# Dilated attention: masked keys give their place to the neighbouring block's keys, two row tiles per turn, the farthest keys merged in the last pass

## The chip, the cores and the metric

The kernel runs on one core of a Trainium2 chip. The metric is the time of one execution on the device in microseconds (us), the median of several runs. "Granted clock" is the share of TensorE's full speed that the chip granted in a stretch.

## The reference

One layer of a decoder with two parallel branches on 2048 tokens of width 1024. Cut to what matters here:

```python
z = rmsnorm(h) @ w_in                  # q | k | v | gate_b | u | v_a | gate_a
q, k = rope(rmsnorm(q)), rope(rmsnorm(k))          # 8 heads of 64
for window, r in ((128, 1), (512, 4), (2048, 16)):  # dilation r
    # query t sees keys t - r*j for j = 0 .. window/r = 128, where they exist
    scores = where(band, q @ [k_prev | k_own].T / 8, -1e30)
    out, lse = softmax(scores) @ [v_prev | v_own], logsumexp(scores)
o = sum over the three of softmax(lse) * out
mixed = concat(o * silu(gate_b), gmlp(u, v_a) * silu(gate_a))
h = h + mixed @ w_out
h = h + sigmoid(rmsnorm(h) @ w_ple_gate + b) * (p @ w_ple_proj)
```

Within a residue class of the dilation the tokens lie in blocks of 128. Query i of a block sees keys 0 to i of its own block and keys i to 127 of the block before. So there are 129 keys, and the one at position i of the block before is the farthest. With dilation 16 there is one block per class and no block before.

## The kernel before

Everything is float32 in accuracy: each operand of a product is split into a high and a low part, and three products are summed. The work is cut into 16 row tiles of 128 tokens and goes in three passes; the results between the passes go through DRAM.

**Pass 1** (`prep`, `step`, `post_qk`, `post_v`, `post_gb`) normalises each row tile, turns it and projects it to q, k, v and gate_b: 24 matmuls of 512 columns each per group. q and k are scaled and rotated (buffers `m1`, `m2`, two of each; `sq`, one), split to fp16 and stored; v is stored as fp16 parts.

**Pass 2** is the attention, with PE's order written by hand. For each pair of heads (`hp`, four of them) and each dilation (`br`, in the order 0, 2, 1), a `Step` does `scores` (TensorE, then the mask, the negated maximum and exp), `turn` (split of the weights to fp16 high and low, one DMA transpose to `pt`) and, `LAG_C` steps later, `values`. A step whose query tile has a block before it has 256 columns of scores per head, two heads, so 512 columns; where there is none, two query tiles share a step. That is 152 steps. Between the steps `fill` places the gMLP branch's products, 1.3 us of them per step. All attention outputs with their denominators and maxima go to `d_o` (`ob` reads them back).

**Pass 3** runs per row tile n: `mixed(n)` (L572) loads the three branches' results (`ob`), the gate product and the gMLP result (`ma`, `mg`) and calls `merge` (L545): DVE works out the weights `w` and scales `ob`, POOL adds the three branches and multiplies by the gate into `ma`. `turn_mixed` (L587) turns `mg` and then `ma` by DMA through the buffer `tm` and splits the result to `aT`. `out_proj(n)` (L596) does 48 matmuls and adds to `xt`. `norm3(n)` (L904) normalises `xt` into `xn`, turns it through `turned` in place (`norm_T` L206, `turn_rows` L197, `turn_words` L172: ACT copies out of `xn`, the DMA transposes back into `xn`, DVE copies out of `xn`) and splits the result. `gate(n)` (L909) does the last 60 matmuls and stores. Tiles 0 and 1 are turned by TensorE and not by DMA.

The order of instructions on each engine and queue in passes 1 and 3 is set by a planner that may issue what is ready ahead of what stands before it in the program. Tiles of one name in one pool share that name's buffers: a new one takes a buffer over from an older one when all that touches the older one is done. `xn`, `ob`, `ma`, `mg`, `tm` and `turned` have one buffer each. The loop of pass 3, in the order of the program:

```python
        for n in range(NT):
            if n + 1 < NT:
                out_proj(n + 1)
            if n + 1 < NT:
                norm3(n + 1)
                load_p(n + 1)
            if n + 2 < NT:
                prep3(n + 2)      # mixed(n + 2), turn_mixed(n + 2)
            gate(n)
```

Of the kernel before, what the change touches and what calls it, by code (L numbers as in the profile page):

```python
# [13 lines left out]
I32 = mybir.dt.int32  # L14
U16 = mybir.dt.uint16
# [4 lines left out]
S = 2048  # L20
# [16 lines left out]
def _shape_constants():  # L37

    p = np.arange(128)

    def mask(keys, back=False):
        keep = keys[None, :] >= p[:, None] if back else keys[None, :] <= p[:, None]
        return np.where(keep, 0, NEG).astype(np.float32)
    k0 = p.reshape(32, 4).T.reshape(128)
    return {"c_ident": np.eye(128, dtype=np.float32),
            "c_mask": np.concatenate([mask(k0, True), mask(k0), mask(p, True), mask(p)], 1),
            "c_freq": INV_FREQ.reshape(1, 32)}
# [3 lines left out]
PR, PH, OB, SV = 3, 6, 5, 5  # L51

LAG_B, LAG_C = 1, 6

BLOCK0, FILL = 18, 1.3
# [26 lines left out]
def hybrid_layer(ctx: ExitStack, tc: tile.TileContext, io, out):  # L82
# [11 lines left out]
    d_qk = [dram.tile([128, HEADS, S], F16, name=f"d_{n}") for n in "qk"]  # L94
# [3 lines left out]
    d_gb = dram.tile([S, 512], F32, name="d_gb")  # L98
    d_at = dram.tile([NT, 128, D], F32, name="d_at")
# [5 lines left out]
    cst.tile([128, 16], F32, name="pad")  # L105
# [163 lines left out]
    with ExitStack() as s1, ExitStack() as s1q:
# [90 lines left out]
        def v_scale():  # L360
# [3 lines left out]
            ones = p1.tile([128, 128], F32, name="ones")  # L364
# [37 lines left out]
        def post_qk(n, which, ps):  # L402
# [17 lines left out]
            nc.vector.tensor_tensor(r, r, rs[:, :, None].to_broadcast([128, HEADS, 64]), op=OP.mult)  # L420
            hl = p1.tile([128, HEADS, 2, 64], F16, name="hl", bufs=2)
# [4 lines left out]
        def turn_qk(n, which, hl):  # L426
# [8 lines left out]
            nc.sync.dma_start(d_qk[which][:, :, n * 128:(n + 1) * 128], st)  # L435

        def post_v(n, ps):
# [4 lines left out]
            nc.scalar.activation(vt[:, :, 0, 0:64], z, AF.Copy, scale=sv)  # L442
            nc.vector.scalar_tensor_tensor(vt[:, :, 1, 0:64], z, sv, vt[:, :, 0, 0:64],
# [513 lines left out]
```

## Time and profile before

| | us |
|---|---|
| three runs | 1290.10, 1296.17, 1296.32 |
| median | 1296.17 |
| the profiled execution | 1295.01 |
| its span, first to last instruction | 1293.2 |
| TensorE's granted clock over the span | 0.976 |
| busy over the span: PE / DVE / ACT / POOL | 1201.3 / 888.2 / 648.9 / 512.1 |

The profile's page gives busy times, a map of 40 slices and the chain that ended last. Times in the rows are microseconds from the start of the span. A row of the timeline is one instruction or a run of equal ones: start, length, engine, line, operation, what it writes and reads. "Idle before" in square brackets is how long the engine had waited and for whom.

### The profile page before, as it was taken

Reading aid. Unit: us, or ns where it says so; the run is one execution under the profiler, and the core shown is the slowest. Engines: PE = TensorE matmul, PEld = TensorE weight load, DVE = VectorE, ACT = ScalarE, POOL = GpSimd, SP = SyncE. Lnnn points to the kernel's source line nnn. Section 1 sums busy time; section 2 is a strip of 40 time slices with the busy share of each in tenths; the row PEclk is TensorE's granted clock in tenths of the full one; section 3 lists DMA queues with packets and bytes.
Section 4 is the critical chain, followed back from the end, with each engine's and each line's share of the span. In section 5 each row is a group of like instructions: output and inputs, shape, how many; then the busy total and the mean of one; then the engine's idle time right before and its main releaser. Section 6 shows DMA issues by size and latency. Waiting matters only on the chain.

```text
span 1293.2 us, 21329 instructions
## 1 busy us (share of the span) xinstructions
PE 1201.3 (93%) x7166; PEld 976.0 (75%) x7166; DVE 888.2 (69%) x2253; ACT 648.9 (50%) x1273; POOL 512.1 (40%) x454
## 2 busy tenths in 40 slices
PE   5999999989995799899799799879999999999998
PEld 4778877767884687687687688768778888888887
DVE  5885565655575678778778678598766766666733
ACT  5754334334344577677677677444334434434422
POOL 4852343433453456555555565342212121221100
PEclk9999999999997899899999999989999999999999
DMA  7598777776769899999999999955555655654531
GB/s 263 160 229 197 168 183 166 165 180 157 175 171 239 202 202 220 219 216 236 218 217 223 219 229 215 207 176 174 141 147 123 165 156 128 153 162 127 143 90 49
DMA packets 442254, 233.21 MB, mean 180 GB/s; under 512 B 337440, under 2 KB 392864, under 8 KB 442144
## 3 DMA queue, kind: packets, MB, share of 16 engines
q1 hardware_dynamic: 442144, 231.85, 75.4%
q8 instruction: 56, 0.92, 0.3%
q14 instruction: 54, 0.44, 0.1%
HBM read 102.66 MB, written 57.28 MB: 124 GB/s over the span
## 4 chain that ended last, share of the span: by engine, by line
PE 41%; DMA 19%; DVE 16%; ACT 7%; issue 7%; POOL 6%; SPq 4%; DVEq 0%; ACTq 0%; POOLq 0%
PE mm L227 17%; PE mm L627 8%; PE gt L227 5%; DMA pt<-raw 4%; DMA xt<-raw 3%; PE s L227 3%; DMA st<-hl 3%; PE s L755 3%; PE pt L791 2%; DVE aT L194 2%; DMA ob<-d_o 2%; ACT raw L179 2%; POOL rsh L148 2%; DVE m L420 1%; DVE pr L758 1%
## 5 line engine op out<-in xcount | busy, mean ns | idle before, releaser
L227 PE MATMUL mm<-wslot,aT 128*128 128x512 f32 x1536 | 362.8, 392 | 7.8 <-ACT aT L193 3.3
L227 PEld LDWEIGHTS mm<-wslot,aT 128*128 128x128 f32 x1536 | 289.4, 189 | 70.4 <-ACT aT L193 4.6
L627 PE MATMUL mm<-wslot,aT 128*128 128x512 f32 x1152 | 317.9, 418 | 23.2 <-DVE raw L618 14.2
L627 PEld LDWEIGHTS mm<-wslot,aT 128*128 128x128 f32 x1152 | 214.1, 197 | 63.5 <-DVE raw L618 14.6
L114 POOL TENSOR_TENSOR raw<-pr,raw 128x512 f16<-128x512 f32 (+1 forms) x152 | 178.0, 1177 | 151.6 <-ACT raw L773 137.9
L766 ACT ACTIVATE pr<-pr,ost 128x256 f32<-128x256 f32 (+1 forms) x384 | 150.5, 451 | 78.8 <-DVE ost L764 70.9
L227 PE MATMUL gt<-wslot,aT 128*128 128x512 f32 x744 | 177.8, 393 | 6.1 <-DVE gb L452 5.3
L227 PEld LDWEIGHTS gt<-wslot,aT 128*128 128x128 f32 x744 | 139.8, 189 | 38.0 <-DVE gb L452 7.0
L791 PEld LDWEIGHTS <-pt 128*128 128x128 f16 x1800 | 66.3, 99 | 62.1 <-issue 33.7
L773 ACT ACTIVATE raw<-pr 128x512 f16<-128x512 f32 (+1 forms) x152 | 93.2, 620 | 39.6 <-DMA pt<-raw 37.4
L791 PE MATMUL pt<-sv,pt 128*128 128x65 f16 x1800 | 83.6, 196 | 21.8 <-DMA pt<-raw 21.8
L758 DVE CUSTOM_DVE_ANT_0 pr<-s,mask 128x256 f32<-128x256 f32 (+1 forms) x256 | 81.3, 359 | 29.7 <-POOL raw L114 16.0
L227 PE MATMUL av<-wslot,aT 128*128 128x512 f32 x360 | 86.0, 392 | 7.3 <-DVE gb L452 6.3
L227 PE MATMUL s<-wslot,aT 128*128 128x512 f32 x384 | 90.0, 390 | 1.6 <-POOL wslot L135 1.6
L114 POOL TENSOR_TENSOR m<-m,m 128x512 f32<-128x512 f32 x32 | 47.9, 1498 | 94.8 <-DVE rsh L147 88.8
L227 PEld LDWEIGHTS av<-wslot,aT 128*128 128x128 f32 x360 | 67.2, 188 | 23.6 <-DVE gb L452 7.9
L227 PEld LDWEIGHTS s<-wslot,aT 128*128 128x128 f32 x384 | 72.0, 188 | 17.0 <-POOL wslot L135 2.0
L755 PEld LDWEIGHTS <-sq 128*128 128x128 f16 x768 | 70.4, 121 | 13.7 <-issue 7.4
L755 PE MATMUL s<-sk,sq 128*128 128x256 f16 (+1 forms) x512 | 73.7, 279 | 7.0 <-DMA sk<-d_k 6.1
L566 POOL TENSOR_TENSOR ma<-ob,ma 128x512 f32<-128x512 f32 x16 | 24.5, 1533 | 122.1 <-DMA ma<-d_gb 58.0
L563 POOL TENSOR_TENSOR ob<-ob 128x512 f32<-128x512 f32 x16 | 21.0, 1314 | 126.5 <-DVE ob L561 126.5
L764 DVE TENSOR_SCALAR ost<-ost 128x2 f32<-128x2 f32 (+1 forms) x152 | 66.9, 442 | 2.6
(209 smaller groups left out, 1723.4 us busy)
## 6 DMA issues: line engine op xcount, KB each, us to landing
xt<-x SPq DMA_DIRECT2D x32, 512.0 KB, 4.6
d_o<-ost SPq DMA_DIRECT2D x48, 264.0 KB, 3.2
raw<-w_in SPq DMA_DIRECT2D x38, 256.0 KB, 3.7
sv<-d_vt SPq DMA_DIRECT2D x32, 264.0 KB, 3.5
ob<-d_o SPq DMA_DIRECT2D x16, 528.0 KB, 4.6
xt<-d_at SPq DMA_DIRECT2D x16, 512.0 KB, 5.0
out<-th SPq DMA_DIRECT2D x32, 256.0 KB, 2.8
d_at<-raw SPq DMA_DIRECT2D x28, 256.0 KB, 2.5
```

Source lines behind the costliest of these rows:

```text
L114: nc.gpsimd.tensor_tensor(dst, a, b, op=op)
L148: nc.gpsimd.tensor_tensor(dst, dst, mhalf[:, :width], op=OP.pow)
L179: nc.scalar.activation(turned[t].bitcast(U16), words[:, t], AF.Copy)
L194: nc.vector.tensor_tensor(lo, f, hi.bitcast(F32), op=OP.subtract)
L227: nc.tensor.matmul(ps, aT[:, ha, k, :], w(slot, hw, k), start=(n == 0), stop=(n == 3 * nk - 1))
L627: nc.tensor.matmul(ps, GT[c][:, ha, k, :], slots[g][:, hw, k, :], start=(n == 0), stop=(n == 23))
L755: nc.tensor.matmul(ps[:, c:c + nk], cols(br, j, Q[h]), cols(br, j, K, n, h, self.nb), start=(n == 0), stop=(n == 1))
L758: nc.vector.tensor_tensor_reduce(pr[:, c:c + nk], ps[:, c:c + nk], mask[:, m - nk:m], -1.0, 3e38, op0=OP.add, op1=OP.min, accum_out=o[:, j ...
L764: nc.vector.tensor_scalar(nm, nm, math.log(PSCALE), None, op0=OP.add)
L766: nc.scalar.activation(pr[:, c:c + nk], pr[:, c:c + nk], AF.Exp, bias=o[:, j - j0, 130 + h:131 + h], scale=-1.0)
L773: nc.scalar.activation(ph, pr[:, :width], AF.Copy)
L791: nc.tensor.matmul(PO[0][:, j % 2, h], self.pt[:, t, c // 128], vt[:, h, vv, 0:65], start=(n == 0), stop=(n == 3 * self.nb - 1))
```

## The change

The scores of a query tile with a block before it are still computed for 256 keys per head, but the keys of its own block that the mask excludes are overwritten in PSUM with the scores of the same positions in the block before (`copy_predicated`). So one tile of 128 keys per head holds all keys but the farthest. Two query tiles now make one `Pair`, with one split and one DMA transpose of 512 weights. For the values the turned weights must be parted again: an AND on DVE with a table of bits gives the own block's share (`pc`), a subtraction on POOL leaves the neighbour's share in `pt`; this comes `LAG_P` = 6 steps behind, five tiles behind the pair, and the values come 9 steps behind. All scores steps have one query tile: 192 of them, 96 pairs, of which 56 are parted. The gMLP filling per step is 0.9 us (no block before) or 1.13 us.

The farthest key's score is a plain dot product: `far_scores` in pass 1 multiplies q with the k of 1 and of 4 row tiles before on POOL and sums on DVE. For this k and v are also stored in float32 (`d_kr`, `d_vr`). `merge` in pass 3 takes these two as two more branches: `mixed` loads the two v tiles into `vr`, POOL multiplies each by its weight and adds it. `vr` takes the buffer of `xn`.

`spatial_weights` of the gMLP moves from the start of pass 2 to row tile 3 of pass 1 and goes through DRAM (`d_ws`). q and k lie in DRAM and in `sk` in blocks of 512 tokens, loaded with 4 transfers each instead of 6.

```diff
-PR, PH, OB, SV = 3, 6, 5, 5
-LAG_B, LAG_C = 1, 6
-BLOCK0, FILL = 18, 1.3
+PR, PH, PC, OB, SV = 3, 4, 2, 5, 5
+LAG_B, LAG_P, LAG_C = 1, 6, 9
+BLOCK0, FILL = 18, (0.9, 1.13)
...
+    FAR = 1, 4
...
             nc.vector.tensor_tensor(r, r, rs[:, :, None].to_broadcast([128, HEADS, 64]), op=OP.mult)
+            if which:
+                nc.sync.dma_start(d_kr[n * 128:(n + 1) * 128], f1)
+            RT["qk"[which]] = n, f1
...
+        def far_scores(n):
+            far = small.tile([128, 2, HEADS], F32, name="far", bufs=1)
+            if n < FAR[1]:
+                nc.vector.memset(far, -NEG)
+            for x, back in enumerate(FAR):
+                if n >= back:
+                    t = p1.tile([128, HEADS, 64], F32, name="m2", bufs=2)
+                    f = t.rearrange("p h d -> p (h d)")
+                    k = RT["k"]
+                    if n - back == k[0]:
+                        k = k[1]
+                    else:
+                        k = f
+                        nc.sync.dma_start(f, d_kr[(n - back) * 128:(n - back + 1) * 128])
+                    pool_tt(f, k, RT["q"][1], OP.mult)
+                    nc.vector.tensor_reduce(far[:, x], t, axis=AX.X, op=OP.add, negate=True)
+            nc.sync.dma_start(d_far[n], far)
...
             nc.scalar.activation(vt[:, :, 0, 0:64], z, AF.Copy, scale=sv)
+            vr = p1.tile([128, 512], F32, name="sq")
+            nc.scalar.activation(vr, ps, AF.Copy, scale=sv)
+            nc.sync.dma_start(d_vr[n * 128:(n + 1) * 128], vr)
...
         nc.gpsimd.tensor_tensor(o, o, nums[:, 4:8], op=OP.add)
         nc.gpsimd.tensor_tensor(o, o, nums[:, 8:12], op=OP.add)
+        for x, back in enumerate(FAR):
+            if n < back:
+                continue
+            t = vr[:, 512 * x:512 * x + 512].rearrange("p (q h d) -> p q h d", q=4, h=2)
+            nc.gpsimd.tensor_tensor(t, t, w[:, 3 + x][:, :, :, None].to_broadcast([128, 4, 2, 64]), op=OP.mult)
+            nc.gpsimd.tensor_tensor(o, o, t, op=OP.add)
         m = mx.rearrange("p (q h d) -> p q h d", q=4, h=2)
         nc.gpsimd.tensor_tensor(m, o, m, op=OP.mult)
...
         nc.sync.dma_start(mx[0], d_gb[rows])
-        merge(ob, mx[0])
+        vr = pm.tile([128, D], F32, name="xn")
+        for x, back in enumerate(FAR):
+            if n >= back:
+                nc.sync.dma_start(vr[:, 512 * x:512 * x + 512], d_vr[(n - back) * 128:(n - back + 1) * 128])
+        merge(ob, mx[0], n, vr)
...
+        class Pair:
+            def turn(self):
+                pr = self.pr.rearrange("p i h k -> p (i h k)")
+                hl = stage().bitcast(F16).rearrange("p (t c) -> p t c", t=2)
+                nc.scalar.activation(hl[:, 0], pr, AF.Copy)
+                pool_tt(hl[:, 1], pr, hl[:, 0], OP.subtract)
+                pt = p2.tile([128, 8, 128], F16, name="pt", bufs=PH)
+                nc.sync.dma_start_transpose(pt, hl.rearrange("p t c -> p (t c)"))
...
+            def part(self, br, after):
...
+                with tc.issue_after(after.ins):
+                    nc.vector.tensor_tensor(d, a, bits[:, None, None, m:m + 64].to_broadcast([128, 2, 2 * n, 64]),
+                                            op=OP.bitwise_and)
+                pool_tt(a, a, d, OP.subtract)
...
+                top = o[:, j - j0, 130:132]
+                if nb == 2:
+                    own = ps[:, :, 128:256]
+                    nc.vector.copy_predicated(own, m.bitcast(U32)[:, None].to_broadcast([128, 2, 128]),
+                                              ps[:, :, 0:128])
+                    nc.vector.tensor_reduce(top, own, axis=AX.X, op=OP.max, negate=True)
...
+                self.last = nc.vector.tensor_scalar(top, top, math.log(PSCALE), None, op0=OP.add)
+                for h in range(2):
+                    nc.scalar.activation(pr[:, h], own[:, h], AF.Exp, bias=top[:, h:h + 1],
+                                         scale=1.0 if nb == 2 else -1.0)
...
+                    for w, v in zip((self.pair.pc, self.pair.pt) if self.nb == 2 else (self.pair.pt,), self.v):
```

## Rows read from the trace of the kernel before

**Rows 1.** The page's map of 40 slices, TensorE's line (tenths busy).

```profile
PE   5999999989995799899799799879999999999998
```

**Rows 2.** Table by stretch: length, busy time and count per engine, clock, DMA share, GB/s.

```profile
0.00:400.00 400.00, 370.32 (x1602) 300.69 (x1602) 253.05 (x454) 183.78 (x312) 183.18 (x173) 1.00 0.75 187
400.00:424.40 24.40, 10.43 (x44) 8.30 (x44) 15.45 (x26) 9.96 (x17) 5.55 (x5) 0.72 0.80 231
424.40:830.00 405.60, 375.51 (x3564) 301.03 (x3564) 311.79 (x1205) 277.88 (x622) 233.61 (x204) 0.97 1.04 217
...
981.20:1250.50 269.30, 269.30 (x1190) 223.07 (x1189) 177.95 (x338) 108.58 (x197) 50.10 (x42) 1.00 0.55 143
```

**Rows 3.** Timeline of PE in pass 3: matmul groups of tiles 1, 2, 7 and 15.

```profile
925.42 1.03 PE L155 MATMUL pt<-ident,xn 128*128 128x128 f32 x8
...
929.88 5.16 PE L227 MATMUL mm<-wslot,aT 128*128 128x512 f32 x22
...
1054.64 5.60 PE L227 MATMUL mm<-wslot,aT 128*128 128x512 f32 x24
1060.08 5.60 PE L227 MATMUL gt<-wslot,aT 128*128 128x512 f32 x24
...
1250.48 5.60 PE L227 MATMUL mm<-wslot,aT 128*128 128x512 f32 x24
```

**Rows 4.** Timeline of the same turn of pass 3: from the residual sum to `xn`'s last reader.

```profile
1065.72 0.69 DVE L602 TENSOR_TENSOR xt<-gt,xt 128x512 f32<-128x512 f32 x1 [1.23 <-PE gt L227]
...
1068.44 0.76 DVE L214 TENSOR_SCALAR xn<-xt,rs 128x1024 f32<-128x1024 f32 x1 [0.66 <-POOL rs L148]
...
1071.47 2.59 SPq L181 DMA_TRANSPOSE xn<-turned  x2
...
1075.72 1.39 DVE L183 COPY turned<-xn 128x1024 uint16<-128x1024 uint16 x2 [0.47 <-DMA xn<-turned]
```

**Rows 5.** The same timeline: from `ma` to the split that out_proj reads.

```profile
1067.50 1.13 ACT L179 ACTIVATE tm<-ma 128x512 uint16<-128x512 uint16 x2
...
1072.61 0.81 DVE L183 COPY tm<-ma 128x512 uint16<-128x512 uint16 x2 [0.76 <-ACT th L917]
...
1073.89 0.76 DVE L194 TENSOR_TENSOR aT<-tm,aT 128x256 fp32r<-128x256 f32 x2
```

**Rows 6.** Groups by line and form, POOL: busy us, mean ns, then idle before.

```profile
L114 POOL TENSOR_TENSOR m<-m,m 128x512 f32<-128x512 f32 x32 | 47.9, 1498 | 94.8 <-DVE rsh L147 88.8 <-DVE m L415 5.4 <-ACT hl L422 0.5
...
L566 POOL TENSOR_TENSOR ma<-ob,ma 128x512 f32<-128x512 f32 x16 | 24.5, 1533 | 122.1 <-DMA ma<-d_gb 58.0 <-DVE turned L183 44.1 <-DVE aT L194 19.9
...
L563 POOL TENSOR_TENSOR ob<-ob 128x512 f32<-128x512 f32 x16 | 21.0, 1314 | 126.5 <-DVE ob L561 126.5
```

**Rows 7.** DMA issues: count, KB each, median us from issue to landing.

```profile
ma<-d_gb SPq DMA_DIRECT2D x16, 256.0 KB, 2.8
```

**Rows 8.** Timeline around 906: the one buffer `tm` changes its user.

```profile
888.29 0.34 SPq L582 DMA_DIRECT2D mg<-d_oa  x1
...
905.41 0.68 DVE L135 TENSOR_TENSOR wslot<-tm,wslot 128x512 fp32r<-128x512 f32 x1
906.11 0.33 SPq L127 DMA_DIRECT2D tm<-w_ple_gate  x1
...
913.06 1.15 ACT L179 ACTIVATE tm<-mg 128x512 uint16<-128x512 uint16 x2 [1.51 <-DVE wslot L135]
```

**Rows 9.** Waits of PE in pass 1 (100 to 400): total, times, longest.

```profile
PE av L227 <- DVE gb L452: 6.3, 4, 2.2
```

**Rows 10.** Waits of PE in pass 2 (440 to 820), same columns.

```profile
PE pt L791 <- DMA pt<-raw: 21.4, 13, 5.8
```

**Rows 11.** Groups by line and form, DVE; the first of 546 to 743.7 only.

```profile
L194 DVE TENSOR_TENSOR aT<-xt,aT 128x512 fp32r<-128x512 f32 x12 | 16.0, 1355 | 0.0
...
L764 DVE TENSOR_SCALAR ost<-ost 128x2 f32<-128x2 f32 x112 | 50.7, 455 | 1.8
...
L423 DVE TENSOR_TENSOR hl<-m,hl 128x512 f16<-128x512 f32 x32 | 22.6, 705 | 9.1 <-ACT hl L422 9.1
```

**Rows 12.** Timeline of PE at the start of pass 2, behind a long wait.

```profile
413.10 7.19 PE L627 MATMUL mm<-wslot,aT 128*128 128x512 f32 x24 [14.19 <-DVE raw L618]
```

More of the change, by code (lines that the diff above doesn't have):

```diff
@@ L92, in hybrid_layer @@
     dram = ctx.enter_context(tc.tile_pool(name="dram", bufs=1, space=bass.MemoryType.DRAM))
-    d_qk = [dram.tile([128, HEADS, S], F16, name=f"d_{n}") for n in "qk"]
+    d_qk = [dram.tile([128, 4, HEADS, 512], F16, name=f"d_{n}") for n in "qk"]
+    d_ws = dram.tile([128, 512], F32, name="d_ws")
     d_vp = dram.tile([S, HEADS * 132], F16, name="d_vp")
@@ L98, in hybrid_layer @@
     d_gb = dram.tile([S, 512], F32, name="d_gb")
+    d_vr = dram.tile([S, 512], F32, name="d_vr")
+    d_kr = dram.tile([S, 512], F32, name="d_kr")
+    d_far = dram.tile([NT, 128, 2, HEADS], F32, name="d_far")
     d_at = dram.tile([NT, 128, D], F32, name="d_at")
@@ L102, in hybrid_layer @@
     d_o = dram.tile([12, S, OW], F32, name="d_o")
-    cst.tile([128, 16], F32, name="pad")
+    cst.tile([128, 8], F32, name="pad")
+    small.tile([128, 64], F32, name="pad", bufs=1)
+    bs = cst.tile([128, 4], F32, name="bs")
     ident = cst.tile([128, 128], F32, name="ident")
@@ L466, in spatial_weights @@
-        def spatial_weights():
-            wsT, gg, bs = pg.tile([128, 4, 128], F32, name="wsT"), CG["gg"], CG["bs"]
-            CG["wsT"] = wsT
-            keep = stage()[:, 0:128]
-            nc.vector.tensor_scalar(keep, CG["mask"][:, 384:512], 0.0, None, op0=OP.is_ge)
-            pt = bank("pt", (128, 4, 128))
+            for name, src in (("mask", io["c_mask"]), ("bits", io["c_bits"]), ("wsT", d_ws),
+                              ("lng", bcast(io["ln_v_g"], 512)), ("lnb", bcast(io["ln_v_b"], 512))):
+                CG[name] = pg.tile([128, {"mask": 256, "bits": 128}.get(name, 512)],
+                                   I32 if name == "bits" else F32, name=name)
+                nc.sync.dma_start(CG[name], src)
@@ L765, in scores @@
[L765 to L781 removed]
+                br, nb, o, j, j0 = self.br, self.nb, self.o, self.j, self.j0
@@ L842, in hybrid_layer @@
                         o = p2.tile([128, 4, OW], F32, name="ost", bufs=OB)
-                    steps.append(Step(br, hp, j0, range(j, j + (2 if first(br, j0 + 3) else 1)), qk, o))
+                    if j % 2 == 0:
+                        pair = Pair()
+                    steps.append(Step(br, hp, j0, j, qk, o, pair))
                     steps[n].scores()
                 if 0 <= n - LAG_B < len(plan):
-                    steps[n - LAG_B].turn()
-                    fill(FILL)
+                    s = steps[n - LAG_B]
+                    if s.i:
+                        s.pair.turn()
+                    fill(FILL[s.nb - 1])
+                if 0 <= n - LAG_P < len(plan) and steps[n - LAG_P].i:
+                    steps[n - LAG_P].pair.part(steps[n - LAG_P].br, steps[min(n, len(plan) - 1)].last)
                 if 0 <= n - LAG_C:
```

197 lines of the change are left out of this document (102 added, 95 removed).

## The prediction

> **What bounds the kernel now.** I read the page's map of 40 slices first [rows 1]: TensorE (PE) is nine or ten tenths busy nearly throughout, with dips at the start, where pass 1 hands over to pass 2, and twice in pass 2. So the kernel is bound by PE, and an edit pays only where PE waits. The table by stretch says how firmly [rows 2]: from 981.20 to 1250.50 PE is busy 269.30 of 269.30 us at granted clock 1.00. In pass 1 it is busy 370.32 of 400, in the handover 10.43 of 24.4, in pass 2 375.51 of 405.6. Pass 2 is the only stage with much to gain (30 us); there the DMA engines' share is 1.04, DVE is busy 311.79 and the clock is 0.97. PE's waits there for turned weights (`pt`) come to 21.4 us in 13 waits [rows 10].
>
> Pass 3 I read from the timeline. out_proj(7) starts at 1054.64 and out_proj(15) at 1250.48 [rows 3]: 195.84/8 = 24.48 us per row tile. Of these out_proj has two groups, the second starting 5.44 behind the first and taking 5.60, so 11.04 us, and gate the other 13.44.
>
> **The change: who holds `xn`'s buffer.** `vr` is a new tile under the name `xn`, which has one buffer. In the program's order a turn of pass 3 is out_proj(n+1), norm3(n+1), which fills and reads `xn`, then prep3(n+2), which loads `vr`, then gate(n). I take it that a name's buffer goes from user to user in the program's order, whatever the planner does with instructions that are ready. The sign for it is `tm`: `mg` of the first row tile was requested at 888.29, yet `tm` came free at 906.09 (905.41 + 0.68), went at 906.11 to a weight load that stands earlier in the program, and held `mg` only at 913.06 [rows 8].
>
> Then pass 3 has a ring. vr(k+1) cannot be loaded until norm3(k) has read `xn` for the last time; norm3(k) needs out_proj(k); and out_proj(k+1) needs the merge that consumes vr(k+1). Before, that merge hung on loads which nothing of tile k held back. One round of the ring, step by step:
>
> - From out_proj's start to `xn`'s last reader: 1054.64 to the end of the residual sum 1066.41 (11.77), then scaling at 1068.44, two DMA transposes at 1071.47, last copy out at 1075.72 + 1.39 = 1077.11 (10.70) [rows 3, 4]. Together **22.47**.
> - The load of `vr`, two transfers of 256 KB. The nearest is the load of `ma`, of the same size, 2.8 us to landing [rows 7]; two of them behind each other with their issue I take as **3.1**, between 2.8 and 4. SP's queue now holds the transfers that stand behind this one (the next `ob`, `mg`, `ma` and the residual's load, the output's store) until `xn` is free; they are needed a round later, so I price that at nothing, and at up to 1 us if a transpose stands behind them.
> - POOL: two products with a broadcast weight, two additions, then the product with the gate. No row shows a broadcast operand on POOL. Nearest is the plain product, 1.498; additions of this size take 1.314, the gate product 1.533 [rows 6]. I take 2 × 1.498 + 2 × 1.345 (between the rows) + 1.533 = **7.22**, with 1.29 to 2.0 for a broadcast product, so 6.8 to 8.2. The first two additions need no `vr` and lie in its shadow.
> - Turning `ma` through `tm` to `aT`: copy at 1067.50, last split ends at 1073.89 + 0.76 = 1074.65 [rows 5]: **7.15**, and 0.2 until the first matmul.
>
> Sum 22.47 + 3.1 + 7.22 + 7.15 + 0.2 = **40.1 us per row tile instead of 24.48**; with the bounds 39.3 to 43. PE then idles behind out_proj. gate's input is ready near 22.47 plus two splits at up to 1.355 [rows 11], so at about 25; gate takes 13.4 from there, to 38.4. That wait also costs speed: behind an idle stretch of 14.19 us the first 24 matmuls took 7.19 instead of 5.60 [rows 12], 1.6 more, so gate ends at 40.0. That just fits. If out_proj too starts cold, the round is 41.7; if POOL's and the load's upper prices come on top, 44.6. Downward, the steps stood beside a full PE and full queues before; take the 1.23, 0.66 and 0.47 of waits ahead of its steps and the 0.76 [rows 4, 5] away and the round is 37.
>
> Now the tiles one by one. out_proj(2) began at 929.88 [rows 3]. The last reader of xn(1) ends at 925.42 + 1.03 = 926.45 (tile 1 is turned by TensorE, so by eight transposes out of `xn`). Tile 2 has only the near far key, so POOL does one product and one addition less, 4.38: 926.45 + 3.1 + 4.38 + 7.15 + 0.2 = 941.3, 11.4 late. Tile 3 is like it and one round of 37.3 later, at 978.6. Twelve rounds of 40.1 then lead to tile 15 at 1459.8 against 1250.48: 209.3 late. What follows out_proj(15) stays, with a colder clock for 2 to 3 us more. **Pass 3: +212**; with the bounds of the round, +174 (37) to +266 (44.6).
>
> **The change: pass 1.** Per row tile there are two products on POOL (1.498 each [rows 6]), two sums on DVE (price not shown; nearest the subtraction of the same 512 elements, 0.705 [rows 11]), one copy on ACT and four transfers of 256 KB at most (`d_kr` out and in, `d_vr` out, and the small `d_far`). The engines have room: DVE is busy 253.05 of 400, ACT 183.78, POOL 183.18, and the DMA share is 0.75 [rows 2]. But the products sit in buffers of `m2` and the copy in `sq`, which the next rotation wants, and PE already waits 6.3 us for evictions on DVE [rows 9]. I take **+8**, a little over once more those waits; 0 if the room hides all, 25 if each of 16 tiles pays one product's 1.5 us. `spatial_weights` moves in here: three loads, a store, four small transposes, inside that figure.
>
> **The change: the handover.** PE is busy 10.43 of 24.4 there, DMA at 231 GB/s [rows 2]. `spatial_weights` leaves it, which frees some DVE and PE work, but the last stores of v, k and far keys and a load of `d_ws` come on the same queue: six transfers of 256 KB at that rate are 6.8 us. I take **+3**, between −1 and +8.
>
> **The change: pass 2.** The count of matmuls is unchanged; turns fall from 152 to 96, all of 512 weights, so a third of the transposes leaves DMA engines whose share is 1.04. That speaks for the 21.4 us of waits [rows 10] getting shorter. Against it: 56 ANDs on DVE, each over 512 words; nearest are the 0.705 and the 1.355 of two-operand instructions [rows 11], so 39 to 76 us; and 40 more steps each with the small scaling at 0.455 [rows 11], 18 us. DVE goes from 311.79 to 369 to 406 of 405.6, so it becomes as full as PE. An AND also waits in DVE's order for a DMA transpose, and behind it stand the maxima of the scores that follow and the gMLP's evictions; `LAG_P` of six steps is there for that. The subtractions on POOL stay 152 (96 + 56). The gain is bounded by 30 (405.6 − 375.51) plus the clock's 3%, so −35; the loss by DVE's overflow and the added waits, +25. I take **−3**, near none, because the relieved resource and the newly filled one stand about equal. The parting behind the last pair adds a DVE and a POOL instruction ahead of the last values: **+2**.
>
> The split by which DVE's price varies has a rule behind it. The L194 instruction, two SBUF operands of 512 elements, takes 1.355 in pass 2, and the equally long L423 in pass 1 takes 0.705; L764, over two elements, still takes 0.455 [rows 11]. The Trainium skill, "GPSIMD Engine Reference", section "1. Specifications", says that VectorE and GpSimd share their SBUF interfaces and get in each other's way when the DVE instruction has two SBUF inputs. By it the ANDs, all with two SBUF inputs, cost the 76 us of the upper price and not the 39; the trace agrees with it as far as the doubled instruction shows, and the second rival below is what it would give.
>
> **Sum.** The profiled execution took 1295.01, about 1 us under the median. 1295 + 8 + 3 − 3 + 2 + 212 = 1517, with 1 for the median **1518 us**. Ends: 1296 + 0 − 1 − 35 + 2 + 174 = 1436 and 1296 + 25 + 8 + 25 + 2 + 266 = 1622.
>
> **Rivals.** (A) *`vr` is loaded out of turn.* If the buffer may go to vr(k+1) before xn(k), the ring is open: `aT` was ready at 1074.65 in a period of 24.48 [rows 5], and the five POOL instructions fit. Pass 3 stays PE-bound and pass 2 decides: 1296 + 8 + 3 − 35 + 2 ≈ **1274**, faster. It decides from the point where the load of `vr` precedes the write of `xn` of the tile ahead. For it: planned loads do run ahead in this kernel. Against it: [rows 8]. (B) *Open ring, DVE the bound of pass 2*: ANDs at 1.355, 76 + 18 on 311.79 make 406, and at PE's present fill of 0.926 the stage needs about 438, +32: **about 1335**; with the ANDs at the lower price it is within a few us of before. (C) The change doesn't do what it says: the ANDs wait for transposes and DVE stands still, so that fewer turns bring no shorter waits; that lies in the +25 above.
>
> **How the numbers follow.** The ring 0.83, because the one thing it needs shows in [rows 8]; open with DVE as the bound 0.05 (slower), open and within 0.5% 0.03, open and relieved 0.09. Faster 0.09, same 0.03, slower 0.88; 0.5% is about what a measurement of this kernel can tell from no change. The range 1420 to 1620 takes in the bounds of the ring, some us more below for steps that an idle pass shortens further, and leaves out the open ring.
>
> **What would show it.** In pass 3 of the changed kernel: out_proj starting every 40 us, PE about 60% busy there at a clock under 1.00, each load of `vr` issued right behind the last copy out of `xn`, POOL idle until `vr` lands. In pass 2: shorter waits for `pt`, a fuller DVE. Wrong would be a pass 3 at 24.5 us per tile (then A or B), or a round well under 37, a part of the path costed twice.

## The result

The changed kernel takes **1557.28 us** (median of 4 runs) against 1294.97 before; the ratio of the means is 1.204, with a 95% interval of 1.201 to 1.206. It is slower by 262 us, where the forecast was 222 (1518 against 1296).

In what follows PE is TensorE and PEld its weight loads, DVE is VectorE, ACT is ScalarE, POOL is GpSimd, and SPq is the queue of SyncE that issues the transfers. The two profiled executions by stage (start or end of the named work, us from the span's start):

| | before | after | later by |
|---|---|---|---|
| pass 2's first scores | 424.41 | 434.22 | 9.8 |
| pass 2's last values end | 830.49 | 830.24 | −0.3 |
| out_proj(0) starts | 886.73 | 877.61 | −9.1 |
| out_proj(2) starts | 928.84 | 938.35 | 9.5 |
| out_proj(15) starts | 1250.48 | 1509.57 | 259.1 |
| span | 1293.2 | 1555.1 | 261.9 |

Up to pass 3 the change gains 9 us. Pass 3 loses 271. The page's map of 40 slices of the changed kernel shows it, TensorE's busy tenths and its granted clock (beside [rows 1], where pass 3 was nines):

```profile
PE   6889999999699999899998887665555577655568
...
PEclk9999999999899999999999988877777888777789
```

The table by stretch of the changed kernel (length, busy time and count of PE, PE's weight loads, DVE, ACT and POOL, clock, DMA share, GB/s), to be read beside [rows 2]: first pass 2, then ten rounds of pass 3, then one round cut into five.

```profile
434.20:830.00 395.80, 375.51 (x3598) 296.48 (x3599) 358.38 (x1087) 224.21 (x567) 243.83 (x204) 0.99 0.84 188
...
1067.40:1509.57 442.17, 277.28 (x1080) 220.37 (x1080) 155.38 (x345) 99.82 (x180) 89.16 (x80) 0.81 0.33 90
...
1155.69:1161.40 5.71, 5.71 (x13) 4.47 (x14) 3.17 (x7) 1.44 (x3) 2.22 (x2) 0.50 0.37 92
1161.40:1167.90 6.50, 6.50 (x30) 5.36 (x29) 0.91 (x2) 0.00 (x0) 0.35 (x1) 0.99 0.12 40
1167.90:1173.00 5.10, 5.10 (x24) 4.24 (x23) 0.69 (x1) 0.00 (x0) 0.00 (x0) 1.00 0.00 0
1173.00:1184.40 11.40, 10.47 (x45) 8.00 (x44) 7.27 (x13) 5.93 (x10) 0.55 (x1) 1.00 0.26 69
1184.40:1200.06 15.66, 0.00 (x1) 0.00 (x1) 3.61 (x14) 2.65 (x7) 5.82 (x5) 0.64 0.56 161
```

In pass 2 PE is busy 375.51 us as before (with 34 matmuls more), but now in 395.80 and not in 405.6, with the DMA share down from 1.04 to 0.84 and DVE up from 311.79 to 358.38. In pass 3 PE is busy 277 of 442 us: 63%. The round of 44.4 us is 28.7 us of work, nearly without a gap, and 15.66 in which PE does nothing.

The same round in the timeline (start, length, engine, line, what it writes and reads; in brackets the idle time ahead and who ended it; out_proj and gate are now L239, the copies of the turning L195 and L191, the far merge L624 and L625):

```profile
1155.69 1.22 PE L239 MATMUL mm<-wslot,aT 128*128 128x512 f32 x2 [15.65 <-ACT aT L205]
1156.71 1.05 PE L239 MATMUL gt<-wslot,aT 128*128 128x512 f32 x2
1157.57 10.43 PE L239 MATMUL mm<-wslot,aT 128*128 128x512 f32 x37
1167.83 5.15 PE L239 MATMUL gt<-wslot,aT 128*128 128x512 f32 x22
1168.03 0.69 DVE L667 TENSOR_TENSOR xt<-mm,xt 128x512 f32<-128x512 f32 x1 [5.62 <-PE mm L239]
1172.82 7.64 PE L239 MATMUL mm<-wslot,aT 128*128 128x512 f32 x33
...
1173.02 0.69 DVE L667 TENSOR_TENSOR xt<-gt,xt 128x512 f32<-128x512 f32 x1 [4.30 <-PE gt L239]
...
1182.77 1.39 DVE L195 COPY turned<-xn 128x1024 uint16<-128x1024 uint16 x2 [0.20 <-DMA xn<-turned]
...
1184.19 0.80 SPq L648 DMA_DIRECT2D xn<-d_vr  x2
...
1187.01 2.09 POOL L624 TENSOR_TENSOR xn<-xn,w 128x512 f32<-128x512 f32 x2 [11.29 <-DMA xn<-d_vr]
1189.06 2.60 POOL L625 TENSOR_TENSOR ob<-ob,xn 128x512 f32<-128x512 f32 x2
1191.74 1.26 POOL L627 TENSOR_TENSOR ma<-ob,ma 128x512 f32<-128x512 f32 x1
...
1193.03 1.15 ACT L191 ACTIVATE tm<-ma 128x512 uint16<-128x512 uint16 x2 [7.84 <-POOL ma L627]
...
1200.06 1.22 PE L239 MATMUL mm<-wslot,aT 128*128 128x512 f32 x2 [15.78 <-ACT aT L205]
```

Read it as a ring. The last copy out of `xn` ends at 1184.16; the load of `vr` is issued at 1184.19; POOL has waited 11.29 us for it; its last product ends at 1193.00; ACT starts turning `ma` at 1193.03; out_proj starts at 1200.06, 44.37 after the one before. Each of these waits only for the one ahead of it. The five steps stand against the forecast's terms like this:

| step | forecast | measured |
|---|---|---|
| out_proj's start to the end of the residual sum | 11.77 | 18.02 |
| norm3 up to `xn`'s last reader | 10.70 | 10.45 |
| load of `vr` | 3.1 | 2.85 |
| POOL | 7.22 | 5.99 |
| turning `ma` to the first matmul | 7.35 | 7.06 |
| round | 40.1 | 44.37 |

One term is wrong, by 6.25 us, and the count of matmuls says why. Between 1155.69 and 1172.98 there are 2 + 2 + 37 + 22 = 63, not out_proj's 48: 15 matmuls of the gate before (it has 48 of this length, and 33 follow) stand inside out_proj's first group, for the sum over that group (L667 on `mm`) waits until 1168.03. At the 0.233 us of one at full clock (5.60 for 24, [rows 3]) they are 3.5 us. The other 2.6 are the clock: 63 at 0.233 are 14.7, and they took 17.3, with a granted clock of 0.50 over the first 5.7 us behind the idle stretch (the lower of TensorE's two levels, 1.2 and 2.4 GHz) and 0.99 after that.

### The profile page after: what moved, and what is told of

Read it like the earlier page. It is cut to its first block, busy times and chain, and to the rows that moved or that the text cites. A ratio compares the mean times of both kernels' runs of the same rounds, so it can differ in the third digit from the quotient of the medians.

```text
span 1555.1 us, 21500 instructions
## 1 busy us (share of the span) xinstructions
PE 1246.4 (80%) x7166; PEld 994.4 (64%) x7166; DVE 950.4 (61%) x2228; ACT 607.0 (39%) x1233; POOL 613.8 (39%) x535
## 4 chain that ended last, share of the span: by engine, by line
PE 29%; DMA 19%; DVE 18%; POOL 9%; issue 6%; ACT 6%; SPq 4%; DVEq 0%; POOLq 0%; ACTq 0%
PE mm L239 11%; PE mm L692 7%; PE gt L239 5%; DMA ob<-d_o 3%; SPq L193 3%; DMA xn<-d_vr 2%; DMA xn<-turned 2%; PE pt L878 2%; DMA raw<-raw 2%; POOL ob L625 2%; PE s L851 2%; DMA st<-hl 2%; ACT turned L191 2%; POOL xn L624 2%; DVE aT L206 2%
## 5 line engine op out<-in xcount | busy, mean ns | idle before, releaser
L239 PE MATMUL mm<-wslot,aT 128*128 128x512 f32 x1536 | 395.8, 416 | 222.5 <-ACT aT L205 215.8
L239 PEld LDWEIGHTS mm<-wslot,aT 128*128 128x128 f32 x1536 | 309.9, 203 | 298.8 <-ACT aT L205 223.4
L692 PE MATMUL mm<-wslot,aT 128*128 128x512 f32 x1152 | 323.9, 416 | 19.3 <-DVE gv L683 9.6
L692 PEld LDWEIGHTS mm<-wslot,aT 128*128 128x128 f32 x1152 | 208.8, 195 | 56.5 <-DVE gv L683 10.2
L239 PE MATMUL gt<-wslot,aT 128*128 128x512 f32 x744 | 190.4, 409 | 10.3 <-DVE rs L159 5.8
L239 PEld LDWEIGHTS gt<-wslot,aT 128*128 128x128 f32 x744 | 147.0, 199 | 45.1 <-DVE gb L495 8.2
L126 POOL TENSOR_TENSOR raw<-pr,raw 128x512 f16<-128x512 f32 x96 | 115.8, 1206 | 53.0 <-ACT raw L808 42.2
L126 POOL TENSOR_TENSOR m<-m,m 128x512 f32<-128x512 f32 x59 | 84.1, 1430 | 103.1 <-DVE rsh L159 90.9
L160 POOL TENSOR_TENSOR rs<-rs,mhalf 128x1 f32<-128x1 f32 x32 | 21.8, 680 | 244.2 <-DVE rs L159 242.6
L205 ACT ACTIVATE aT<-tm 128x256 fp32r<-128x256 f32 x56 | 20.8, 414 | 207.3 <-PE gt L239 195.9
L126 POOL TENSOR_TENSOR pt<-pt,pc 128x512 int32<-128x512 int32 (+1 forms) x56 | 69.5, 1241 | 76.7 <-issue 21.6
L239 PE MATMUL s<-wslot,aT 128*128 128x512 f32 x384 | 91.1, 392 | 1.5 <-POOL wslot L147 1.5
L624 POOL TENSOR_TENSOR xn<-xn,w 128x512 f32<-128x512 f32 x27 | 28.1, 1056 | 159.8 <-DMA xn<-d_vr 156.6
L239 PE MATMUL av<-wslot,aT 128*128 128x512 f32 x360 | 86.7, 393 | 0.8 <-ACT wslot L145 0.6
L239 PEld LDWEIGHTS s<-wslot,aT 128*128 128x128 f32 x384 | 72.6, 189 | 17.1 <-POOL wslot L147 1.9
L865 DVE TENSOR_SCALAR ost<-ost 128x2 f32<-128x2 f32 x192 | 80.0, 418 | 3.7
L239 PEld LDWEIGHTS av<-wslot,aT 128*128 128x128 f32 x360 | 67.6, 189 | 16.4 <-ACT wslot L145 1.0
L867 ACT ACTIVATE pr<-pr,ost 128x128 f32<-128x128 f32 x168 | 57.0, 393 | 49.9 <-DVE ost L865 43.3
```

Source lines behind the costliest of these rows:

```text
L126: nc.gpsimd.tensor_tensor(dst, a, b, op=op)
L239: nc.tensor.matmul(ps, aT[:, ha, k, :], w(slot, hw, k), start=(n == 0), stop=(n == 3 * nk - 1))
L624: nc.gpsimd.tensor_tensor(t, t, w[:, 3 + x][:, :, :, None].to_broadcast([128, 4, 2, 64]), op=OP.mult)
L692: nc.tensor.matmul(ps, GT[c][:, ha, k, :], slots[g][:, hw, k, :], start=(n == 0), stop=(n == 23))
L865: self.last = nc.vector.tensor_scalar(top, top, math.log(PSCALE), None, op0=OP.add)
L867: nc.scalar.activation(pr[:, h], own[:, h], AF.Exp, bias=top[:, h:h + 1], scale=1.0 if nb == 2 else -1.0)
```

## The experiments

Besides their times, all are compared by the same two marks of the trace. "Pass 2" is from its first scores to the end of its last values, "rest" from there to the end of the span. The marks are those of one profiled execution each; e2 and e3 were run once, so their times are single ones.

| | median us | first scores | pass 2 | rest |
|---|---|---|---|---|
| before | 1293 to 1295 | 424.4 | 406.1 | 462.7 |
| the change | 1557.3 | 434.2 | 396.0 | 724.9 |
| e2, only the ring added to before | 1555.8 | 421.7 | 404.5 | 727.9 |
| e3, gate ahead of out_proj | 1491.7 | 432.1 | 398.1 | 659.8 |
| e1, merge ahead of norm3 | 1330.8 | 433.0 | 396.5 | 498.5 |
| e4, no far merges | 1290.6 | 433.4 | 396.5 | 457.0 |
| e5, `vr` in its own buffer | 1334.6 | 441.9 | 396.8 | 497.0 |
| e6, e5 with spatial_weights at tile 8 | 1337.4 | 439.2 | 394.1 | 503.0 |
| e10, e5 without the POOL work | 1300.7 | 439.5 | 394.4 | 462.9 |
| e11, e5 without the loads | 1335.5 | 439.1 | 396.3 | 495.9 |
| e12, e5 without the gate's load | 1325.8 | 436.5 | 396.3 | 490.7 |
| e7, e4 with transposes doubled | 1336.4 | 437.4 | 438.5 | 459.7 |
| e8, e4 without the parting | 1268.6 | 435.0 | 368.9 | 462.6 |
| e9, e4 without far scores | 1291.3 | 426.7 | 398.4 | 464.1 |

### Is the ring enough? (e2)

The kernel before, with this in `mixed` and the products in `merge`:

```diff
+        vr = pm.tile([128, D], F32, name="xn")
+        for x, back in enumerate((1, 4)):
+            if n >= back:
+                nc.sync.dma_start(vr[:, 512 * x:512 * x + 512], d_gb[(n - back) * 128:(n - back + 1) * 128])
+        merge(ob, mx[0], n, vr)
```

> The kernel before, with only the ring added in pass 3: vr under the name xn, two loads of 256 KB from gate_b's rows and two products and two additions on POOL, at the place where the changed kernel has them. It adds numbers that the reference doesn't have. Theory of the ring: rounds of about 44 us and a time of about 1295 + 255 = 1550. Rival, that passes 1 and 2 of the change or its clock there carry a good part of the loss: rounds under 38 and a time under 1480.

1555.8 us, within 2 us of the whole change. The timeline of PE in this kernel (columns as above) has the rounds:

```profile
1108.95 1.22 PE L227 MATMUL mm<-wslot,aT 128*128 128x512 f32 x2 [15.86 <-ACT aT L193]
...
1153.32 1.22 PE L227 MATMUL mm<-wslot,aT 128*128 128x512 f32 x2 [15.88 <-ACT aT L193]
```

The period is 44.37, the same as in the changed kernel. So the ring, with the POOL work in it, accounts for all of the loss, and passes 1 and 2 for none of it.

### Where do the 6.25 us of out_proj go? (e3)

```diff
         for n in range(NT):
+            gate(n)
             if n + 1 < NT:
                 out_proj(n + 1)
...
-            gate(n)
```

> The changed kernel with gate(n) before out_proj(n+1) in the program instead of behind prep3(n+2), so that TensorE's 13.4 us of gate lie in the wait and out_proj comes right behind them. Theory, that the 4.3 us by which a round is longer than forecast are out_proj at the lower clock after the wait (17.3 instead of 11.0 us): out_proj takes 11.0 again, the ring itself is 38.1, and the round ends between that and 40 (25 for gate's input, then gate at the lower clock for its first matmuls): a time of about 1490 to 1505. Rival, that the longer round comes from DVE, the queue or the loads: out_proj's starts stay 44 apart, the time near 1557.

1491.7 us, 66 less than the change. PE's timeline in this kernel:

```profile
1119.09 12.90 PE L239 MATMUL mm<-wslot,aT 128*128 128x512 f32 x48 [9.87 <-ACT aT L205]
...
1135.10 0.73 PE L239 MATMUL mm<-wslot,aT 128*128 128x512 f32 x2 [1.75 <-ACT aT L205]
...
1141.81 4.47 PE L239 MATMUL gt<-wslot,aT 128*128 128x512 f32 x19
...
1173.32 0.74 PE L239 MATMUL mm<-wslot,aT 128*128 128x512 f32 x2 [2.00 <-ACT aT L205]
```

The long wait is now ahead of gate, whose 48 matmuls pay for the clock (12.90 where two groups of 5.60 would be 11.2). out_proj runs from 1135.10 to 1146.28, 11.2 us, and the round is 38.2. That is the picture the forecast had drawn. But the expectation named only the clock, and this run takes away both things at once, gate's 15 matmuls inside out_proj's first group and the lower clock; that they are 3.5 and 2.6 us comes from the count above, not from this run.

### Is the loss gone when the ring is open? (e1, e4, e5)

e1 moves the merge:

```diff
+            if n + 2 < NT:
+                mixed(n + 2)
             if n + 1 < NT:
                 norm3(n + 1)
                 load_p(n + 1)
             if n + 2 < NT:
-                prep3(n + 2)
+                turn_mixed(n + 2, p3)
```

e4 leaves `vr` and its products out:

```diff
-            if n < back:
+            if vr is None or n < back:
...
-        merge(ob, mx[0], n, vr)
+        merge(ob, mx[0], n, None)
```

e5 gives `vr` another name:

```diff
-        vr = pm.tile([128, D], F32, name="xn")
+        vr = pm.tile([128, D], F16, name="vr")
```

> The changed kernel with one step of pass 3 moved in the program: the merge of tile n+2 (with its load of vr) stands before norm3(n+1) instead of behind it, so vr takes xn's buffer over from a tile one round older. Nothing is left out. Theory of the ring: out_proj then starts every 24.5 us again instead of 44.4, and the time is about 1285 (tile 0's out_proj 9 us earlier than before, then pass 3 as long as before), within 1275 to 1300. Rival, that the merges of the far keys are themselves too much for POOL, DMA or DVE: the round stays at 30 us or more, and the time over 1380.

> The changed kernel without vr: pass 3 loads no far values and leaves out the far keys' products and additions (their weights stay in the denominators, so the far keys' share of the output is missing). Theory of the ring: 24.5 us per tile, about 1283, and within 4 us of the run with the merge moved, since the far merges have room beside TensorE. Rival, that the far merges cost by themselves: over 8 us faster than the run with the merge moved.

> The changed kernel with vr in a buffer of its own, so that it neither waits for norm3 nor holds ob back; the program's order is the changed kernel's. To make room, v of the far keys is stored and merged in fp16 and the gate's bias is kept in fp16 (both are smaller in accuracy, nothing is left out). Theory: what the merge-moved run (1331) still lost, against 1291 without far merges, is the time that POOL holds ob while it waits for vr, and DVE's queue behind the late ob. Then the round is 24.5 and the time 1288 to 1296. Rival, that POOL's four extra instructions and their loads cost DVE or the queue time wherever vr lies: rounds over 25.5 and a time over 1305.

None of the three came out as expected. e4 took 1290.6 us, a ratio to before of 0.997 (0.995 to 0.999): without the far merges the whole loss is gone. But it is not within 4 us of e1, it is 40 faster, which was its rival: the far merges cost by themselves. e1 took 1330.8, e5 1334.6. Both open the ring, for most of their rounds are 26 to 29 us and not 44, yet not 24.5. The expectations had counted POOL's work as room beside PE.

In e1 one sees a late `ob`. Timeline of that kernel:

```profile
1097.12 2.23 POOL L624 TENSOR_TENSOR xn<-xn,w 128x512 f32<-128x512 f32 x2 [7.16 <-DMA xn<-d_vr]
...
1103.93 0.37 SPq L639 DMA_DIRECT2D ob<-d_o  x1
...
1108.94 0.19 DVE L600 TENSOR_REDUCE mn<-ob 128x8 f32<-128x24 f32 x1 [4.31 <-DMA ob<-d_o]
...
1109.91 0.75 DVE L206 TENSOR_TENSOR aT<-tm,aT 128x256 fp32r<-128x256 f32 x2
...
1118.01 0.73 PE L239 MATMUL mm<-wslot,aT 128*128 128x512 f32 x2 [1.21 <-ACT aT L205]
```

POOL still waits for `vr`, holds `ob` until 1103.9, so the next `ob` is loaded then, and DVE stands 4.31 us in front of it with the split of `mg` queued behind. e5 was to take this away: its `vr` is loaded in time. It made nothing better (its rival again, over 1305), so the late `ob` alone is not the cause.

### POOL's work or the loads? (e10, e11, e12)

All three start from e5. e10 cuts the products and additions:

```diff
-            t = vr[:, 512 * x:512 * x + 512].rearrange("p (q h d) -> p q h d", q=4, h=2)
-            nc.gpsimd.tensor_tensor(t, t, w[:, 3 + x][:, :, :, None].to_broadcast([128, 4, 2, 64]), op=OP.mult)
-            nc.gpsimd.tensor_tensor(o, o, t, op=OP.add)
+            t = vr[:, 512 * x:512 * x + 4]
+            nc.gpsimd.tensor_tensor(o[:, 0, 0, 0:4], o[:, 0, 0, 0:4], t, op=OP.add)
```

e11 drops the loads:

```diff
-            if n >= back:
-                nc.sync.dma_start(vr[:, 512 * x:512 * x + 512], d_vr[(n - back) * 128:(n - back + 1) * 128])
...
+            v = bple[:, 512 * x:512 * x + 512].rearrange("p (q h d) -> p q h d", q=4, h=2)
+            nc.gpsimd.tensor_tensor(t, v, w[:, 3 + x][:, :, :, None].to_broadcast([128, 4, 2, 64]), op=OP.mult)
```

e12 drops the gate's load:

```diff
-        nc.sync.dma_start(mx[0], d_gb[rows])
...
-        nc.gpsimd.tensor_tensor(m, o, m, op=OP.mult)
+        nc.gpsimd.tensor_tensor(m, o, nums[:, 4:8], op=OP.mult)
```

> The run with vr's own buffer (1334.6), with the loads of vr and the weights, but the products and additions of the far keys cut to four elements each (their values are missing from the output). Theory, that the four POOL instructions (6.0 us per tile, in POOL's queue ahead of norm3's 0.55 us one, and slowing the DVE instructions beside them) make the round 27.4 instead of 24.5: the round is 24.5 and the time 1288 to 1298. Rival, that the loads and the longer row of DVE's small instructions do it: over 1315.

> The run with vr's own buffer (1334.6), with the products and additions at full size, but without the loads of vr: the products read the resident bias instead (so the far keys' part is wrong). Theory of POOL: no loads needed for the loss, 1325 to 1337. Rival, that the loads do it: under 1305.

> The run with vr's own buffer (1334.6), without the load of the gate into ma: the last product on POOL multiplies by a part of ob instead (so the gate is missing). Theory, that the round is a second ring, through ma and ob: ma's copy out, its load (4.1 us), the gate product, ob's load, DVE's merge, mg's split, and ma's copy out again, which had little slack before. Without the load it is 4 us shorter: a round under 25.5, 1290 to 1308. Rival, that it is DVE and norm3 being slowed by POOL whatever ma waits for: over 1320.

By the rest's column e5 has 497.0. Without the loads it is 495.9, without POOL's work 462.9, which is before's 462.7. So POOL's four instructions make 34 us and the loads 1. What is left over e4's 457.0 in e10, 5.9 us, no run accounts for. (e10's total is 2.7 us above the end of its expected range; its first scores came 6 us later than e4's, which has nothing to do with pass 3.) Without the gate's load it is 490.7: the second ring through `ma` is worth 6 us, not the cause.

How POOL's work reaches PE shows in the groups by line and form, DVE and POOL from 1000 to 1250 (busy us, mean ns, then idle before and whom for). First e4, without the far merges:

```profile
L206 DVE TENSOR_TENSOR aT<-tm,aT 128x256 fp32r<-128x256 f32 x40 | 25.3, 672 | 0.0
...
L616 DVE TENSOR_TENSOR ob<-ob,w 128x1536 f32<-128x1536 f32 x9 | 15.8, 1760 | 0.9
...
L226 DVE TENSOR_SCALAR xn<-xt,rs 128x1024 f32<-128x1024 f32 x10 | 7.5, 753 | 6.6 <-POOL rs L160 6.6
```

In the timeline of e4, the two splits of one `mg`:

```profile
1086.06 2.00 DVE L206 TENSOR_TENSOR aT<-tm,aT 128x256 fp32r<-128x256 f32 x2
```

Then the groups of e5, with the far merges, and PE's waits there in the same stretch:

```profile
L206 DVE TENSOR_TENSOR aT<-tm,aT 128x256 fp32r<-128x256 f32 x36 | 31.6, 920 | 0.0
L616 DVE TENSOR_TENSOR ob<-ob,w 128x1536 f32<-128x1536 f32 x9 | 23.7, 2634 | 0.9
...
L226 DVE TENSOR_SCALAR xn<-xt,rs 128x1024 f32<-128x1024 f32 x9 | 6.8, 754 | 24.7 <-POOL rs L160 24.7
...
L624 POOL TENSOR_TENSOR vr<-vr,w 128x512 f16<-128x512 f16 x18 | 32.0, 1801 | 69.8 <-DVE w L613 69.8
...
PE mm L239 <- ACT aT L205: 18.2, 8, 3.4
```

One round of e5 in the timeline, DVE and POOL (the third row is the second of the first row's two products, by itself):

```profile
1088.16 3.56 POOL L624 TENSOR_TENSOR vr<-vr,w 128x512 f16<-128x512 f16 x2 [7.83 <-DVE w L613]
1088.19 2.64 DVE L616 TENSOR_TENSOR ob<-ob,w 128x1536 f32<-128x1536 f32 x1
1089.17 2.56 POOL L624 TENSOR_TENSOR vr<-vr,w 128x512 f16<-128x512 f16 x1
1090.74 0.68 DVE L667 TENSOR_TENSOR xt<-mm,xt 128x512 f32<-128x512 f32 x1
...
1091.94 2.77 DVE L206 TENSOR_TENSOR aT<-tm,aT 128x256 fp32r<-128x256 f32 x2
...
1094.51 2.47 POOL L625 TENSOR_TENSOR ob<-ob,vr 128x512 f32<-128x512 f32 x2
...
1096.93 0.55 POOL L160 TENSOR_TENSOR rs<-rs,mhalf 128x1 f32<-128x1 f32 x1
```

Two things at once. DVE's scaling of `ob` (L616) takes 2.634 instead of 1.760, as the far products run beside it. The two engines seem to take turns: the first product takes 1.04, as it does in the changed kernel with DVE idle, and L616 is 0.87 longer; the second product takes 2.56 and ends 0.90 behind L616. The two splits of `mg` to `aT` (L206), beside POOL's additions, take 2.77; in e4 they come later beside the same additions and take 2.00, and with POOL idle two such splits take 0.76 ([rows 5]). And norm3's small POOL instruction (L160) stands behind POOL's longer row: DVE was ready for `rs` at 1094.8 and got it at 1097.5. Over the nine rounds that is 24.7 us, 2.7 each, against 0.66 in e4. In e10, without the products, L616 is back at 1.760. PE feels it through `aT`: its waits from 1000 to 1250 are all for ACT's split, 18.2 us in e5, 17.4 in e11 and none in e4 and e10. How the 34 us divide between the slowed instructions and the later `rs` was not told apart.

The Trainium skill, "GPSIMD Engine Reference", section "1. Specifications", says that VectorE and GpSimd share SBUF interfaces and contend where a DVE instruction has two SBUF inputs. L616 and L206 have two and are slowed; L667, beside the same POOL products but with one input in PSUM, keeps its 0.68. The traces agree with the rule here.

### What set pass 2? (e7, e8)

e7 doubles transposes:

```diff
-                nc.sync.dma_start_transpose(pt, hl.rearrange("p t c -> p (t c)"))
+                for _ in range(2 if self.wide else 1):
+                    nc.sync.dma_start_transpose(pt, hl.rearrange("p t c -> p (t c)"))
```

e8 leaves the parting out, at the start of `part`:

```diff
-                if not self.wide:
-                    return
+                return
```

> The run without far merges in pass 3 (1290.6), with the DMA transposes of the 56 parted pairs issued twice, to the same tile: 152 of them in pass 2, as many as in the kernel before. Theory, that pass 2 became shorter because fewer transposes left the DMA engines free: TensorE's waits for pt come back and the time is 8 to 18 us longer, 1299 to 1309. Rival, that it became shorter by the other filling and lags, not by the transposes: within 3 us of 1290.6.

> The run without far merges in pass 3 (1290.6), without the parting in pass 2: no AND on DVE and no subtraction on POOL, the values read pt for both blocks (so the neighbour's and the own block's weights are mixed up). Theory, that the parting lies beside TensorE's work: only its waits for POOL (8.9 us) and DVE (4.0 us) in pass 2 can go, so 0 to 13 us faster, 1278 to 1291. Rival, that DVE, at 358 of 396 us, set pass 2's end: 20 us faster or more.

Table by stretch, 440 to 825 of each kernel (columns as before): e4, e7, e8.

```profile
440.00:825.00 385.00, 364.53 (x3480) 287.36 (x3480) 350.82 (x1063) 220.03 (x556) 238.24 (x201) 0.99 0.84 187
```

```profile
440.00:825.00 385.00, 341.10 (x3137) 265.02 (x3136) 317.21 (x969) 202.28 (x509) 214.93 (x180) 0.95 0.97 204
```

```profile
440.00:825.00 385.00, 378.84 (x3630) 301.52 (x3628) 322.62 (x1043) 227.62 (x574) 179.08 (x153) 1.00 0.90 199
```

With 56 transposes more, pass 2 is 42 us longer (438.5 against 396.5), far over the 18 that the theory allowed at most. PE's waits (line, for whom, total us, times, longest) are hardly for the transposes themselves (2.5 us in e7) but for the parting behind them:

```profile
PE pt L875 <- POOL pt L126: 20.6, 22, 1.2
PE pt L875 <- DVE pc L821: 10.5, 12, 1.7
```

against 8.9 and 4.0 in the changed kernel, where the wait for the DMA ([rows 10]) fell to 0.4:

```profile
PE pt L878 <- POOL pt L126: 8.9, 10, 1.1
PE pt L878 <- DVE pc L824: 4.0, 5, 1.2
...
PE pt L878 <- DMA pt<-raw: 0.4, 1, 0.4
```

A doubled transpose also makes the AND behind it wait for the second copy, and DVE stops with it, so the 42 us are an upper price of 56 transposes in this arrangement. Leaving the parting out makes pass 2 27.6 us shorter and PE busy 378.84 of 385 us. The time is 22 us shorter, which is the rival's side of the line: the parting is not hidden beside PE, though PE's waits named only 12.9 us for it. The DVE group of e4 shows what one AND took:

```profile
L820 DVE TENSOR_TENSOR pc<-pt,bits 128x512 int32<-128x512 int32 x51 | 35.9, 704 | 0.2 <-DMA pt<-raw 0.2
```

Whether the AND on DVE or the subtraction on POOL (1.24 us each, the other half of the parting) costs more was not tried.

### Pass 1 (e9, e6)

e9, from e4:

```diff
-            if which:
-                nc.sync.dma_start(d_kr[n * 128:(n + 1) * 128], f1)
...
-            if n < FAR[1]:
-                nc.vector.memset(far, -NEG)
+            nc.vector.memset(far, -NEG)
...
-                if n >= back:
+                if n < 0:
...
-            nc.sync.dma_start(d_vr[n * 128:(n + 1) * 128], vr)
```

e6, from e5:

```diff
-            if n == 3:
+            if n == 8:
                 spatial_weights()
```

> The run without far merges in pass 3 (1290.6), without the far scores in pass 1 either: far_scores only stores a constant, and k and v of the far keys are not stored in float32 (the far keys are missing altogether). Pass 2's first scores came 9 us later in that run than before (433.4 against 424.4). Theory, that far_scores and its transfers are most of it: 4 to 8 us faster, 1283 to 1287. Rival, that it is spatial_weights at row tile 3 (5.0 us of wait) and the handover's loads: within 3 us of 1290.6.

> As the run with vr's own buffer, and spatial_weights at row tile 8 of pass 1 instead of row tile 3. Theory, that its loads and DVE work hold up the turning of a row tile early in pass 1 (TensorE waited 5.0 us there in the changed kernel, in a stretch with no slack): 4 to 6 us faster than the run before it, about 1286. Rival, that the wait only moves to tile 8 or into the handover: within 2 us.

Without far scores pass 2 begins at 426.7 and not 433.4, so they are 6.7 us of the 9 by which it had become later. But the time is 1291.3 against 1290.6, where the rival had put it, though not for the rival's reason: what was won was given back in the rest, 464.1 against 457.0. Nor does the time show e6's 2.7 us at the first scores. And the wait that e6 was to remove is still there, in PE's timeline of that kernel:

```profile
85.51 2.07 PE L239 MATMUL mm<-wslot,aT 128*128 128x512 f32 x4 [4.79 <-ACT aT L205]
```

With `spatial_weights` five row tiles later it still stands at 85.5 us (4.97 at 85.58 in e5), so that step is not its cause; in e9 it is gone, so it comes from the far keys' work. My reading of it was wrong. Why the tail of the gMLP and pass 3 give such gains back was not settled; every edit in pass 1 also lets the planner place what follows anew.

## Why the prediction was right, and where it was wrong

**The ring: right.** The step on which it hung, that `vr` gets `xn`'s buffer only after norm3 of the tile before, as `tm` went from user to user [rows 8], holds in all rounds. Opening it (e5) takes away 223 of the 262 us, leaving the merges out (e4) takes away all of them, and the ring with its merges added to the kernel before (e2) makes the whole loss.

**The round: 40.1 forecast, 44.4 measured; the term that failed is out_proj.** I had taken its 11.04 us over from a busy PE [rows 3] and put the wait ahead of gate, so that gate would pay 1.6 us for the clock, which "just fits". But gate(k−1) has had its input since the round before and follows out_proj(k) directly. The whole wait lies in one piece behind gate, and out_proj is what comes next: it pays for the clock (2.6 us) and has 15 of gate's matmuls inside its first group (3.5 us). The case "if out_proj too starts cold, 41.7" had 1.6 of these 6.1. POOL came cheaper (5.99 for 7.22): a product with the broadcast weight took 1.04 us, below the lower bound of 1.29 that I had taken from the plain instructions. The plain product's 1.498 [rows 6] was a mean of two kinds: 13 of those 32 took 1.28 to 1.30, the others 1.41 to 1.76. Counted from out_proj(0), the net error over tiles 3 to 15 is 12 × 4.0, and 11 us came in at tiles 2 and 3; that is the 59 us by which pass 3 was longer than the 209 forecast for out_proj(15).

**Pass 1 and the handover: right in sum, +11 forecast, +9.8 measured.** Far scores are most of it (e9).

**Pass 2: the sign was right and the size was not; −1 forecast, −19 measured up to out_proj(0)** (−10 within pass 2 and −9 in what of the gMLP was left behind it). "Near none, because the relieved resource and the newly filled one stand about equal" hides two large terms: the parting at 28 us and the fewer transposes, at up to 42. The bound of −35 by PE's idle time and the clock did hold, though its two parts, 30.1 and 3% of 375.51, make 41. DVE did not become as full as PE: it was busy 358.38 us, under even the forecast's 369, and the AND cost 0.704 us, the lower of the two prices. By the rule of the Trainium skill ("GPSIMD Engine Reference", "1. Specifications") rival B had given it the upper one, 1.355; the measurement decides. It hardly tests the rule, for 45 of the changed kernel's 56 ANDs had POOL busy beside them for less than a tenth of their time. Of the nine that stood mostly beside a POOL instruction, eight took 0.68 to 0.70 and one 1.66.

**Rival A: its time was wrong.** With the ring open it gave 1274, since "the five POOL instructions fit". They fit POOL's time, and the two runs with an open ring still took 1331 and 1335. The mechanism, DVE slowed by POOL and norm3's small POOL instruction behind the far products, stood in no rival. That rival B's "about 1335" lies beside them is chance: it put the loss into pass 2, which took 397 us in both and not 438 (and its own terms, 1296 + 8 + 3 + 32 + 2, make 1341). Had the buffer gone out of turn, the change would by e1 and e5 have been 3% slower all the same.

The two misses, 59 us too little in pass 3 and about 18 too much in pass 2, are opposite, so the sum of 1518 is off by less (39) than the larger of them: that part of the agreement is luck.

**Two small slips in the working.** out_proj(2) began at 928.84 in the kernel before, not at 929.88: two matmuls of each group run ahead of the 22 read there. The lower bound of the round adds up to 39.4, not 39.3. Neither bears on the result.

## What to carry to other kernels

A second user under a one-buffer name is a dependency: follow it around the loop, from the buffer's release to what it feeds, and see whether that comes back to the release; if so, the loop's period is the sum of the latencies, however idle every engine is. When a wait is priced, look up which instruction comes first behind it and what the order puts between its parts. And room on an engine is not enough: ask what stands behind the added instructions in its queue, and which instructions of its neighbour run beside them.

## What the runs showed of the hardware that was not expected

- After 15.7 us without work PE's granted clock was 0.50 (1.2 of 2.4 GHz) over the next 5.7 us of matmuls and 0.99 to 1.00 from there: 2.6 us lost in the round shown.
- DVE's scaling of 128x1536 elements takes 1.760 us, and 2.634 while POOL's products run beside it. Of POOL's two products there the first takes 1.04 and the second 2.56; in the changed kernel, with DVE idle, both take 1.04. It looks as if one engine waits while the other's instruction runs; the products are fp16 here and float32 there, and the first one's 1.04 is the same.
- That product, 128x512 float32 with a broadcast second operand, is cheaper at 1.04 us than the plain one of the same round, the product with the gate (L627), at 1.26.
- The AND of 128x512 32-bit words on DVE took 0.704 us on average, mostly with POOL idle beside it.
